# A Conformer and dilated-attention decoder on one core: Silu results moved from PSUM to SBUF, the last feature tile's taps and the weight splits shared out anew

## The chip, the cores and the metric

The kernel runs on one core of a Trainium2 chip. The metric is the time of one execution in microseconds on the device, lower is better. All times below are microseconds (us) unless marked ns. The engines are PE (TensorE; PEld is its weight load), DVE (VectorE), ACT (ScalarE), POOL (GpSimd) and SP, which only issues the DMAs here.

## What is computed

256 tokens of width 2048 go through two layers. Layer 0 is a Conformer convolution layer and a squared-ReLU MLP, layer 1 a dilated attention layer and another MLP; a shared K/V projection stands between them. All in float32. The change touches the convolution layer alone, apart from one scheduling priority that the attention's output product shares:

```python
def conformer_conv(y, w_in, b_in, w_dw, b_dw, ln_g, ln_b, w_out, b_out):
    u = y @ w_in + b_in                      # 2048 -> 4096
    a, gate = jnp.split(u, 2, axis=-1)
    u = a * jax.nn.sigmoid(gate)
    u = depthwise_causal_conv(u, w_dw) + b_dw   # 31 taps per feature
    u = jax.nn.silu(layernorm(u, ln_g, ln_b))
    return u @ w_out + b_out
```

## The kernel before

Everything lies transposed: 128 features on the partitions, the 256 tokens along the free axis, so the width of 2048 is KT = 16 feature tiles. Weights come as 128x2048 tiles of 1 MB, one per output tile. To keep float32 accuracy on the fast float32r path, a weight tile `raw` is split: ACT casts it to `hi` (line 138), DVE or POOL subtracts to get `lo` (line 140). `split_upto(n)` does this for the tiles up to number n of a fixed list `order` (32 tiles of w_in, then 16 of w_out at 32 to 47, then the MLP and so on). The set POOL_LO says whose `lo` POOL makes; the rest is DVE's. The pool `wp` has 11 buffers for raw, hi and lo together, so a new split waits until a product has released an older tile. Activations are split in the same way (`split_into`, lines 219 to 221). A product (`product`, lines 188 to 195) is, per K tile, one 128x512 matmul with `hi` and one 128x256 matmul with `lo`: a pair.

**The convolution stage** (loop over c at line 397). For each feature tile c PE makes two products with w_in, value (`pa`) and gate (`pg`), of 48 matmuls each; ACT makes sigmoid(pg) (line 417), DVE makes u (line 418), and `conv` makes the 31 taps: some products on ACT (line 323) that POOL adds in part (line 332) and DVE sums by TENSOR_REDUCE (line 355), the rest as a chain on DVE (lines 344 to 349). For the last tile, 15, PE takes 18 taps with diagonal matrices (line 311; each matmul is two rows of the trace), ACT 7, DVE 6. `center` subtracts a shift from a finished tile (line 382) and ACT squares it (line 384); `statistics` lets PE sum the columns of tiles and squares (128x1 matmuls, line 236). In iteration c it stands between the value and the gate product. After the last tile come mean, variance and its root, spread over the partitions by four PE transposes (line 247) into `norm`.

**Silu and w_out.** For each c DVE normalizes (lines 477, 478), ACT applies Silu (line 480) into `s`, a tile of the PSUM pool `psp`, which has 8 buffers in all, and `split_into` makes the activation tile. Then `project` multiplies with w_out: the first N0 = 4 output tiles (call them f0 to f3) go together over the first LAST = 13 K tiles, each into its own PSUM tile, so that PE can follow the activations as they come; then each of the four is finished alone over the K tiles left, and its residual add is done on DVE (lines 490, 492), its scaled split on ACT and DVE (lines 226, 227), its sum of squares (lines 258, 262). The other 12 output tiles follow one by one. The attention's w_o goes through the same `project`.

The order on each engine is set by a scheduler at build time, which follows the order of the code and `tc.high_priority`. Each engine then works strictly in that order.

## Time and profile before

| | before |
|---|---|
| median of 3 runs | 2055.55 us (2054.39 to 2055.83) |
| the profiled execution's own time | 2054.33 us |
| its span (first to last instruction) | 2052.1 us |
| busy: PE / PEld / DVE / ACT / POOL | 98% / 87% / 62% / 48% / 11% |
| granted TensorE clock, mean | 0.99 of full |
| DMA, mean over the span | 179 GB/s |

PE is busy for 98% of the span. In the 40 slices of the page only the first, the fifth and the last fall below nine tenths, and the fifth (205 to 257 us) is the lowest, with six: this is where the convolution ends and the product with w_out begins. An idle time in a row stands in square brackets with what ended it. The clock of TensorE has two levels here, 1.00 (2.4 GHz) and 0.50 (1.2 GHz); a value between is a mean over a stretch.

### The profile page before, as it was taken

The page shows a single profiled execution, that of the slowest core. Times are in us where ns is not written, and L with a number is a line of the kernel's source. Part 1 is how long each engine was busy: PE and PEld are TensorE (multiplying, and loading weights), DVE is VectorE, ACT ScalarE, POOL GpSimd, SP SyncE. Part 2 cuts the span into 40 slices and gives each one's busy share as a digit, 9 for nine tenths or more (in the row PEclk, how much of TensorE's full clock was granted, in tenths as well). Part 3 has the DMA queues.
Part 4 walks back from the last instruction along what each step waited for, and adds up shares of the span by engine and source line. Part 5 has one row for each costly group of instructions (what it writes and reads, how often), then busy time and mean ns, then how long its engine had stood idle before and what let it go on. Part 6 is the DMA issues. An engine that isn't in the chain of part 4 may idle for free.

```text
span 2052.1 us, 28638 instructions
## 1 busy us (share of the span) xinstructions
PE 2007.8 (98%) x11958; PEld 1780.7 (87%) x11958; DVE 1281.1 (62%) x1745; ACT 988.3 (48%) x1353; POOL 228.3 (11%) x102
## 2 busy tenths in 40 slices
PE   8999699999999999999999999999999999999997
PEld 7999678888888888888889987888888888888886
DVE  7999666665555555555675565665555555555564
ACT  4888544543453344345454654454344335434452
POOL 2898320000000000000003220000000000000000
PEclk9999799999999999999999999999999999999999
DMA  7454245555555555555555344555555555555551
GB/s 294 146 192 156 68 158 176 201 185 185 188 190 194 187 185 186 188 194 191 185 185 184 145 144 144 185 187 187 195 191 185 185 187 192 191 189 185 187 187 77
DMA packets 51584, 367.42 MB, mean 179 GB/s; under 512 B 5856, under 2 KB 5856, under 8 KB 7552
## 3 DMA queue, kind: packets, MB, share of 16 engines
q1 hardware_dynamic: 51312, 365.60, 51.6%
q8 instruction: 93, 1.52, 0.3%
q14 instruction: 35, 0.29, 0.0%
q10 hardware_dynamic: 144, 0.01, 0.0%
HBM read 363.49 MB, written 2.10 MB: 178 GB/s over the span
## 4 chain that ended last, share of the span: by engine, by line
PE 51%; issue 35%; DVE 2%; ACT 0%; DVEq 0%; POOLq 0%; POOL 0%
PE ps L194 29%; PE ps L195 15%; PE ps L208 1%; PE ps L209 1%; PE ps L210 1%; PE ps L642 0%; DVE lo L140 0%; DVE act L227 0%; PE ps L615 0%; PE ps L614 0%; PE ps L613 0%; PE ps L680 0%; DVE t L262 0%; DVE t L477 0%; DVE t L478 0%
## 5 line engine op out<-in xcount | busy, mean ns | idle before, releaser
L194 PE MATMUL ps<-act,hi 128*128 128x512 f32 x4672 | 1639.1, 395 | 15.4 <-DVE act L221 11.4
L195 PE MATMUL ps<-act,lo 128*128 128x256 f32 x4672 | 1309.7, 281 | 5.3 <-DVE lo L140 3.6
L194 PEld LDWEIGHTS ps<-act,hi 128*128 128x128 f32 x4672 | 876.7, 188 | 219.7 <-DVE act L221 13.1
L138 ACT CAST hi<-raw 128x2048 fp32r<-128x2048 f32 x336 | 640.7, 1909 | 857.1 <-PE ps L194 699.3
L140 DVE TENSOR_TENSOR lo<-raw,hi 128x2048 fp32r<-128x2048 f32 x295 | 678.0, 2298 | 443.0 <-ACT hi L138 441.1
L195 PEld LDWEIGHTS ps<-act,lo 128*128 128x128 f32 x4672 | 884.6, 189 | 7.7 <-DVE lo L140 4.6
L496 DVE TENSOR_TENSOR h<-ps,h 128x256 f32<-128x256 f32 x288 | 119.6, 424 | 195.1 <-PE ps L195 190.9
L140 POOL TENSOR_TENSOR lo<-raw,hi 128x2048 fp32r<-128x2048 f32 x41 | 189.4, 4624 | 142.6 <-ACT hi L138 139.5
L241 POOL TENSOR_TENSOR rc<-ms,neg_half 128x2 f32<-128x2 f32 x5 | 3.6, 728 | 1628.2 <-DVE ms L270 1628.2
L208 PE MATMUL ps<-act,hi 128*128 128x256 f32 x640 | 184.6, 288 | 0.0
L209 PE MATMUL ps<-act,hi 128*128 128x256 f32 x640 | 181.0, 283 | 0.0
L210 PE MATMUL ps<-act,lo 128*128 128x256 f32 x640 | 180.9, 283 | 0.0
L209 PEld LDWEIGHTS ps<-act,hi 128*128 128x128 f32 x640 | 122.5, 191 | 0.5
L208 PEld LDWEIGHTS ps<-act,hi 128*128 128x128 f32 x640 | 122.2, 191 | 0.5
L210 PEld LDWEIGHTS ps<-act,lo 128*128 128x128 f32 x640 | 122.3, 191 | 0.0
L323 ACT ACTIVATE prod<-u,vecs 128x256 f32<-128x256 f32 x217 | 92.4, 517 | 21.3 <-DVE u L418 13.7
L349 DVE SCALAR_TENSOR_TENSOR ps<-u,vecs,ps 128x256 f32<-128x256 f32 x197 | 79.1, 482 | 0.0
L538 ACT ACTIVATE t<-t 128x256 f32<-128x256 f32 x128 | 52.5, 410 | 42.5 <-DVE t L536 42.5
L214 PE MATMUL ps<-act,raw 128*128 128x256 f32 x256 | 57.7, 386 | 6.4 <-DVE act L297 6.4
L214 PEld LDWEIGHTS ps<-act,raw 128*128 128x128 f32 x256 | 49.3, 194 | 13.1 <-DVE act L297 6.4
L221 DVE TENSOR_TENSOR act<-t,act 128x256 fp32r<-128x256 f32 x128 | 53.3, 416 | 7.4 <-ACT act L220 7.4
L200 DVE TENSOR_TENSOR t<-ps,t 128x256 f32<-128x256 f32 x128 | 53.5, 418 | 1.6 <-ACT t L199 1.6
(109 smaller groups left out, 844.4 us busy)
## 6 DMA issues: line engine op xcount, KB each, us to landing
raw<-in_m_in SPq DMA_DIRECT2D x128, 1024.0 KB, 4.8
raw<-in_m_out SPq DMA_DIRECT2D x128, 1024.0 KB, 4.8
raw<-in_w_in SPq DMA_DIRECT2D x31, 1024.0 KB, 4.9
raw<-in_w_out SPq DMA_DIRECT2D x16, 1024.0 KB, 4.8
raw<-in_w_q SPq DMA_DIRECT2D x16, 1024.0 KB, 4.8
raw<-in_w_o SPq DMA_DIRECT2D x16, 1024.0 KB, 4.9
raw<-in_w_k SPq DMA_DIRECT2D x4, 1024.0 KB, 4.9
raw<-in_w_v SPq DMA_DIRECT2D x4, 1024.0 KB, 4.8
```

The costliest lines, as they stand in the source:

```text
L138: nc.scalar.copy(out=hi, in_=raw)
L140: eng.tensor_tensor(out=lo, in0=raw, in1=hi.bitcast(F32), op=ALU.subtract)
L194: nc.tensor.matmul(ps, lhsT=wh, rhs=a.rearrange("p i t -> p (i t)"), start=k == 0, stop=False)
L195: nc.tensor.matmul(ps[:, :T], lhsT=wl, rhs=a[:, 0, :], start=False, stop=k == KT - 1)
L200: nc.vector.tensor_tensor(out=dst, in0=ps[:, :T], in1=dst, op=ALU.add)
L208: nc.tensor.matmul(ps, lhsT=wh, rhs=a[:, 0, :], start=k == 0, stop=False)
L209: nc.tensor.matmul(ps, lhsT=wh, rhs=a[:, 1, :], start=False, stop=False)
L210: nc.tensor.matmul(ps, lhsT=wl, rhs=a[:, 0, :], start=False, stop=k == KT - 1)
L214: nc.tensor.matmul(ps, lhsT=w[:, k * P:(k + 1) * P], rhs=act_of(k), start=k == 0, stop=k == KT - 1)
L323: nc.scalar.activation(out=slot(buf, i), in_=u[:, j:j + T], func=AF.Copy, scale=tap(c, j))
L349: nc.vector.scalar_tensor_tensor(out=a if j < TAPS - 2 else slot(last, i % 2), in0=x, scalar=tap(c, j), in1=a, op0=ALU.mult, op1=ALU.add)
L496: nc.vector.tensor_tensor(out=h[:, f, :], in0=half, in1=h[:, f, :], op=ALU.add)
```

## The change

1. In POOL_LO `range(39)` becomes `range(36)`: the `lo` of tiles 36, 37 and 38 (w_out's f4, f5, f6) goes from POOL to DVE.
2. Tile 15's taps: 16 on PE, 6 on ACT without a POOL add, 9 on DVE (were 18, 7 and 6).
3. From c = 1 on the gate's weight tile is loaded, split and multiplied ahead of the value's, and `statistics` stands behind both products. The set S1_PLAIN (tiles multiplied unsplit) keeps its numbers, so numbers 11 and 28 now name other tiles of the same pairs.
4. `s` comes from the SBUF pool `tp` (7 buffers) and no longer from PSUM.
5. In `project` the splits behind each of the first four tiles get priority 60.
6. For w_out the common K tiles are 11, not 13; for w_o they stay 13.

```diff
@@ constants @@
-POOL_LO = (set(range(39)) - {28}) | set(range(183, 202, 2))
+POOL_LO = (set(range(36)) - {28}) | set(range(183, 202, 2))
-PE_TAPS = {15: (18, [(6, 1)])}
+PE_TAPS = {15: (16, [(6, 0)])}
@@ order of the weights @@
-        order += [(w_in[c], 2 * c not in S1_PLAIN), (w_in[KT + c], 2 * c + 1 not in S1_PLAIN)]
+        pair = [w_in[c], w_in[KT + c]] if c == 0 else [w_in[KT + c], w_in[c]]
+        order += [(w, 2 * c + i not in S1_PLAIN) for i, w in enumerate(pair)]
@@ loop over c @@
+                pg = s1_product(c)
                 pa = s1_product(c)
                 statistics()
-                pg = s1_product(c)
@@ Silu @@
-        s = ps_tile()[:, :T]
+        s = tmp()
         nc.scalar.activation(out=s, in_=z, func=AF.Silu, scale=col("lng", c), bias=col("lnb", c))
@@ project @@
             finish(f, ws[f], pss[f], range(last, KT))
-            split_upto(n_used[0] + LOOK - N0 + f + 1)
+            with tc.high_priority(60):
+                split_upto(n_used[0] + LOOK - N0 + f + 1)
@@ call for w_out @@
-    acts, rms = project(acts, add_bias_residual, "gl0", range(LAST), LAST)
+    acts, rms = project(acts, add_bias_residual, "gl0", range(LAST - 2), LAST - 2)
```

Between lines 87 and 474 the line numbers of the changed kernel are one higher than before.

What the change does to the order, at three places. **PE behind the last product with w_in**, before (line 210 is the product's last matmul, 236 are column sums, of tiles `act` and of squares `t`, 311 the taps of tile 15):

```order
L210 MATMUL ps_2411<-act_475,lo_2287 128x256
L236 MATMUL ps_1888<-ones_d_91,act_2034 128x1 x2
L236 MATMUL ps_1888<-ones_d_91,t_2350 128x1 x2
L236 MATMUL ps_1888<-ones_d_91,t_2501 128x1 x2
L236 MATMUL ps_1888<-ones_d_91,t_2504 128x1 x2
...
L236 MATMUL ps_1888<-ones_d_91,t_2507 128x1 x2
...
L236 MATMUL ps_1888<-ones_d_91,t_2510 128x1 x2
L311 MATMUL ps_2463<-u1_115,act_1864 128x256 x4
```

and in the changed kernel:

```order
L211 MATMUL ps_2398<-act_475,lo_2284 128x256
L237 MATMUL ps_1885<-ones_d_91,t_2341 128x1 x2
L237 MATMUL ps_1885<-ones_d_91,act_2031 128x1 x2
L237 MATMUL ps_1885<-ones_d_91,t_2344 128x1 x2
...
L237 MATMUL ps_1885<-ones_d_91,t_2347 128x1 x2
L237 MATMUL ps_1885<-ones_d_91,t_2497 128x1 x2
L237 MATMUL ps_1885<-ones_d_91,t_2500 128x1 x2
L237 MATMUL ps_1885<-ones_d_91,act_1709 128x1
L312 MATMUL ps_2460<-u1_115,act_1864 128x256 x4
```

Before, the taps stand behind the squares of tiles 8 to 11 (t_2501 to t_2510); now behind those of tiles 8 and 9 only, but also behind sums that stood between the two products of c = 15 before.

**DVE from the u of tile 15 to its finished tile**, before (u0 belongs to tile 14, u1 to tile 15; prod are the ACT products):

```order
L349 SCALAR_TENSOR_TENSOR prod_2304<-u0_114,vecs_73,ps_120 128x256
L355 TENSOR_REDUCE prod_2312<-prod_2304 128x256
L418 SCALAR_TENSOR_TENSOR u1_115<-ps_2352,vecs_73,t_2460 128x256
L355 TENSOR_REDUCE act_2340<-prod_2312 128x256
L344 TENSOR_SCALAR ps_120<-u1_115,vecs_73 128x256
...
L349 SCALAR_TENSOR_TENSOR prod_2482<-u1_115,vecs_73,ps_121 128x256
L355 TENSOR_REDUCE act_2340<-prod_2482 128x256
L358 TENSOR_TENSOR act_2340<-ps_2463,act_2340 128x256
```

and in the changed kernel:

```order
L419 SCALAR_TENSOR_TENSOR u1_115<-ps_2398,vecs_73,t_2457 128x256
L350 SCALAR_TENSOR_TENSOR ps_120<-u0_114,vecs_73,ps_120 128x256
L348 TENSOR_SCALAR ps_121<-u1_115,vecs_73 128x256
...
L350 SCALAR_TENSOR_TENSOR prod_2301<-u0_114,vecs_73,ps_120 128x256
...
L356 TENSOR_REDUCE prod_2309<-prod_2301 128x256
...
L356 TENSOR_REDUCE act_2337<-prod_2309 128x256
...
L356 TENSOR_REDUCE act_2337<-prod_2477 128x256
L359 TENSOR_TENSOR act_2337<-ps_2460,act_2337 128x256
```

The u of tile 15 has moved ahead of three chain steps of tile 14 and of that tile's first TENSOR_REDUCE.

**DVE where f0 to f3 are finished**, before (ps_2704 to ps_2707 are their PSUM tiles):

```order
L490 SCALAR_TENSOR_TENSOR h_75<-ps_2706,vecs_73,h_75 128x256
L227 SCALAR_TENSOR_TENSOR act_2820<-h_75,vecs_73,act_2820 128x256
L492 TENSOR_TENSOR h_75<-ps_2706,h_75 128x256
L490 SCALAR_TENSOR_TENSOR h_75<-ps_2707,vecs_73,h_75 128x256
L492 TENSOR_TENSOR h_75<-ps_2707,h_75 128x256
L227 SCALAR_TENSOR_TENSOR act_2838<-h_75,vecs_73,act_2838 128x256
```

and in the changed kernel (ps_2700 to ps_2703):

```order
L490 SCALAR_TENSOR_TENSOR h_75<-ps_2702,vecs_73,h_75 128x256
L492 TENSOR_TENSOR h_75<-ps_2701,h_75 128x256
L490 SCALAR_TENSOR_TENSOR h_75<-ps_2703,vecs_73,h_75 128x256
L492 TENSOR_TENSOR h_75<-ps_2702,h_75 128x256
L141 TENSOR_TENSOR lo_2809<-raw_2299,hi_2808 128x2048
L228 SCALAR_TENSOR_TENSOR act_2804<-h_75,vecs_73,act_2804 128x256
```

The `lo` of f4 (lo_2809), POOL's before, is now on DVE, behind the line 490 of f3, which reads f3's finished product.

## Rows read from the trace of the kernel before

**Rows 1.** Windows by stage: busy us (count) of PE, PEld, DVE, ACT, POOL; PEclk; DMA.
```profile
50.00:212.50 162.50, 162.50 (x1286) 160.07 (x1285) 156.09 (x293) 137.70 (x259) 143.82 (x67) 1.00 0.46 163
212.50:234.40 21.90, 17.81 (x91) 15.63 (x89) 11.60 (x20) 9.16 (x18) 8.37 (x4) 0.84 0.34 112
234.40:245.70 11.30, 0.00 (x0) 0.00 (x0) 11.23 (x34) 9.84 (x22) 0.00 (x0) 0.51 0.00 0
245.70:271.70 26.00, 25.97 (x129) 21.50 (x129) 8.00 (x21) 8.31 (x15) 1.30 (x1) 0.88 0.05 11
271.70:345.00 73.30, 69.38 (x385) 60.02 (x385) 59.38 (x66) 36.29 (x43) 12.75 (x3) 0.98 0.57 198
```

**Rows 2.** Timeline, 203 to 231 us, all engines: start, us, instruction, [idle before].
```profile
203.88 4.80 DVE L349 SCALAR_TENSOR_TENSOR ps<-u,vecs,ps 128x256 f32<-128x256 f32 x12
...
212.60 0.50 PE L236 MATMUL ps<-ones_d,act 128*128 128x1 f32 x4
...
215.33 0.45 ACT L417 ACTIVATE t<-ps,vecs 128x256 f32<-128x256 f32 x1
...
215.81 0.48 DVE L418 SCALAR_TENSOR_TENSOR u<-ps,vecs,t 128x256 f32<-128x256 f32 x1 [0.26 <-ACT t L417]
216.21 1.74 DVE L355 TENSOR_REDUCE act<-prod 128x256 f32<-128x1536 f32 x1
...
219.96 10.23 PE L311 MATMUL ps<-u,act 128*128 128x256 f32 x36
...
220.84 2.29 DVE L355 TENSOR_REDUCE act<-prod 128x256 f32<-128x2048 f32 x1 [0.15 <-ACT prod L323]
...
230.23 0.42 DVE L358 TENSOR_TENSOR act<-ps,act 128x256 f32<-128x256 f32 x1 [7.11 <-PE ps L311]
```

**Rows 3.** Timeline, 234 to 247 us, start of the product with w_out.
```profile
234.39 0.42 DVE L477 TENSOR_TENSOR t<-act,ps 128x256 f32<-128x256 f32 x1 [0.55 <-PE ps L247]
...
235.90 0.37 ACT L220 CAST act<-ps 128x256 fp32r<-128x256 f32 x1
...
236.31 0.42 DVE L221 TENSOR_TENSOR act<-ps,act 128x256 fp32r<-128x256 f32 x1
...
245.73 0.79 PE L194 MATMUL ps<-act,hi 128*128 128x512 f32 x1 [11.37 <-DVE act L221]
...
246.72 0.79 PE L194 MATMUL ps<-act,hi 128*128 128x512 f32 x1
```

**Rows 4.** Groups of instructions, 0 to 330 us: the same cast read from SBUF.
```profile
L220 ACT CAST act<-act 128x256 fp32r<-128x256 f32 x16 | 5.1, 400 | 0.5 <-DVE act L405 0.5
```

**Rows 5.** Windows of 2 us: TensorE while tile 15's taps run.
```profile
222.00:224.00 2.00, 2.00 (x7) 1.55 (x6) 1.12 (x1) 0.10 (x1) 0.00 (x0) 0.50 0.84 356
```

**Rows 6.** Timeline of DVE, 262 to 345 us.
```profile
271.04 4.19 DVE L227 SCALAR_TENSOR_TENSOR act<-h,vecs,act 128x256 fp32r<-128x256 f32 x1
...
279.89 4.85 DVE L262 TENSOR_TENSOR t<-t 128x256 f32<-128x256 f32 x1
...
286.97 2.28 DVE L140 TENSOR_TENSOR lo<-raw,hi 128x2048 fp32r<-128x2048 f32 x1
...
311.53 0.48 DVE L490 SCALAR_TENSOR_TENSOR h<-ps,vecs,h 128x256 f32<-128x256 f32 x1 [0.69 <-PE ps L195]
...
339.46 0.48 DVE L490 SCALAR_TENSOR_TENSOR h<-ps,vecs,h 128x256 f32<-128x256 f32 x1 [0.69 <-PE ps L195]
```

**Rows 7.** Timeline of POOL, 262 to 345 us.
```profile
270.40 14.05 POOL L140 TENSOR_TENSOR lo<-raw,hi 128x2048 fp32r<-128x2048 f32 x3 [36.75 <-ACT hi L138]
```

**Rows 8.** Timeline of PE, 262 to 300 us: its three waits.
```profile
272.88 0.50 PE L194 MATMUL ps<-act,hi 128*128 128x512 f32 x1 [1.00 <-ACT hi L138]
275.00 0.39 PE L195 MATMUL ps<-act,lo 128*128 128x256 f32 x1 [1.62 <-POOL lo L140]
...
289.31 0.38 PE L195 MATMUL ps<-act,lo 128*128 128x256 f32 x1 [1.30 <-DVE lo L140]
```

**Rows 9.** Timeline of PE, 1250 to 1260 us: product with w_o.
```profile
1254.34 0.39 PE L195 MATMUL ps<-act,lo 128*128 128x256 f32 x1 [2.35 <-DVE lo L140]
```

## The prediction, made before the changed kernel was run

> **What bounds the kernel now.** I read the busy shares by stage first. From 50 to 212.5 us PE is busy all the time at full clock, and so is nearly DVE (156.1 of 162.5 us) [rows 1]; there nothing can be won but by less work. The next two stages, the end of the convolution and the start of the product with w_out, are different: PE is busy 17.8 of 21.9 us and then 0 of 11.3 us, and in that second stretch its clock is the lower level, 0.51 [rows 1]. In the two after them, the product with w_out, PE is busy but for 3.9 us of waits, at clocks of 0.88 and 0.98 [rows 1]. After 345 us PE is the bound again, save one short stretch at w_o. So a gain must come from 212.5 to 345 us, and what matters there is which wait ends last.
>
> I then read the timeline of that stretch, step by step.
>
> *The tail of the convolution.* The sigmoid of tile 15 starts on ACT at 215.33, u on DVE at 215.81, and PE's taps run from 219.96 for 10.23 us, partly at the lower clock (0.50 from 222 to 224 us) [rows 2, 5]. DVE has done its part before and waits 7.11 us for those taps, until 230.23 [rows 2]. PE's taps set the end here.
>
> *The start of w_out.* The first normalizing step runs at 234.39, and the first activation tile is ready when line 221 ends, at 236.31 + 0.42 = 236.73 [rows 3]. Yet PE starts only at 245.73, after 11.37 us of idling that a line 221 on DVE ended [rows 3]. That is not the first line 221 but the tenth: one activation takes 0.99 us, the distance of PE's first two starts (245.73 and 246.72) [rows 3], and 236.73 + 9 x 0.99 = 245.64. The cause is in the code. `psp` has 8 buffers; `norm` holds one, the 16 tiles `s` go around in the other 7, and f0's PSUM tile, which comes after them, takes the buffer of s number 9 (counted from 0), f1's that of number 10, and so on. So PE waits for a buffer, not for data.
>
> *The product with w_out.* Three waits stand here, 1.00, 1.62 and 1.30 us, for `hi`, for POOL's `lo` and for DVE's `lo` [rows 8]. While POOL makes its three `lo` in 14.05 us [rows 7], two DVE steps last 4.19 and 4.85 us [rows 6] that otherwise take about 0.45.
>
> **The change, part by part.**
>
> *Gate first, sums behind both, taps shared anew (edits 2 and 3).* The sigmoid no longer waits for the last product. DVE now reaches u with three chain steps and one TENSOR_REDUCE fewer ahead of it, as the order shows. A chain step costs 4.80 / 12 = 0.40, the long TENSOR_REDUCE 2.29 [rows 2], and 0.26 us of waiting for the sigmoid goes: 215.81 - 0.26 - 3 x 0.40 - 2.29 = 212.1. PE must have finished too: its last product ended by 212.60, and the six column sums (12 matmuls, 0.50 / 4 = 0.125 each [rows 2]) that stood between the two products now stand behind: 212.6 - 1.5 = 211.1. So u starts at 212.1. Behind it DVE has 12 small steps (three of tile 14, nine of tile 15, since its chain grows from 6 taps to 9), 4.8 us, TENSOR_REDUCEs of 2.29, 1.74 and 2.29, and one centering of 0.42: 11.5 us [rows 2]. With 0.4 for u itself, the last TENSOR_REDUCE ends at 224.0. PE's part: 15 column-sum matmuls from 211.1, 1.9 us, and then 16 taps, at worst at the old mean of 10.23 x 16 / 18 = 9.1 us: 222.1. So DVE, not PE, is late next, and the tail is 230.23 - 224.0 = 6.2 us shorter. PE will then have idled some microseconds and may do the last sums and transposes at half clock; I take off 0.5 (12 matmuls at 0.125 more would be 1.5, but most of them wait for data anyway). **Gain 5.7.** Bounds: if u comes as late as now, only the two taps go, 10.23 x 2 / 18 = 1.1; if DVE, which waited for sigmoids before, reaches u as early as PE allows, 7.2. I take the middle way, nearest to the rows of DVE. The ACT products and POOL's adds of tile 15 shrink too; they are hidden, since the last TENSOR_REDUCE needs them some 9 us after u.
>
> *Silu in SBUF (edit 4).* f0's PSUM tile no longer has to wait for an `s`, so PE starts when the first activation is ready: 245.73 - 236.73 = **9.0 gained**. What cover is needed: PE must not run into the activations. PE's four pairs per K tile take 4 x 0.349 = 1.40 us (0.349 from the five output tiles between 311.53 and 339.46, 27.93 / 5 = 5.59 each, 16 pairs [rows 6]), the activations come every 0.99, so PE stays behind. And f1 to f3 no longer start 0.99 apart but one pair apart, about 0.70 at half clock: 3 x 0.29 = **0.9 gained**. The lower clock at the start stays, since PE idles ahead of it in both kernels. `z` and `s` now share 7 buffers, 3.5 tiles deep at 0.99 each, 3.5 us, against 2.34 us from the first step to line 221 [rows 3]: no wait.
>
> What speaks against edit 4: the cast of an activation takes 0.37 us when it reads PSUM [rows 3] and 0.40 when it reads SBUF [rows 4], 0.03 more per tile, for the first tile alone on PE's path. By the Trainium skill, "ScalarE: Activation LUTs", section "Step-by-step: what each stage is for", ScalarE writes faster to PSUM than to SBUF, so that this edit would move Silu to the slower side; it gives no figure, no row here shows a Silu into SBUF, and the sum by it would be the same but for the first tile's Silu.
>
> *Splits of f4 to f6 on DVE, priority, 11 common K tiles (edits 1, 5, 6).* From 271.7 to 345 us PE needs 12 x 5.59 = 67.0 and takes 73.3 [rows 1, 6]: 3.9 of waits and 2.4 that are mostly half clock after the longest of them. With 11 common tiles f0's weights come free 6 pairs (2.1 us) earlier against f3's end, so `hi` of f4 is ready in time. But the order puts f4's `lo` behind f3's line 490 on DVE: f3's end, then 0.48 + 0.42 + 2.28 = 3.2 us [rows 6], of which two hi matmuls cover about 0.4. A wait of 2.8 takes the place of 1.00 + 1.62, so it is 0.2 worse, and the half clock behind it stays. The third wait, 1.30, should go, since POOL no longer holds DVE up (three `lo` cost DVE 3 x 2.28 = 6.8, the two held steps alone gave 8.1 away). **Gain 1.1.** Bounds: all 6.3 if the scheduler's order hurts less than I read it; 2 lost if f5 or f6 waits as well.
>
> *w_o.* Edit 5 acts there too; a wait of 2.35 for DVE's `lo` stands there [rows 9], and the order of `lo` moves by one short step. I take 0, between 1 gained and 1 lost.
>
> **Sum:** 5.7 + 9.0 + 0.9 + 1.1 = 16.7 us. The profiled execution's own time of 2054.33 (span 2052.1) becomes 2037.6; it lies 1.2 under the median of the three runs, 2055.55, which becomes **2038.9 us**.
>
> **The rivals.**
>
> *u stays late.* ACT's queue could still hold the sigmoid behind a cast that waits for a weight buffer, as it does now. Then the tail gains 1.1 only: 1.1 + 9.0 + 0.9 + 1.1 = 12.1, 2043.5 us. Against it: the gate's product now ends a whole product earlier.
>
> *PE's wait is not for the buffer.* If something else releases it, the 9.9 of edit 4 fail and 6.8 remain: 2048.8. Against it: the 0.99 steps of PE's first starts [rows 3].
>
> *POOL holds DVE in the Silu loop.* Line 222 now has both inputs in SBUF, like the two steps that stretched to 4.19 and 4.85 beside POOL [rows 6, 7]. If POOL's last `lo` of the stage slides into the loop, one line 222 waits up to 14.05 / 3 = 4.7: gain 12.0, 2043.6. Against it: the last activation's weights were split long before 234 us, POOL being busy 8.4 us in that stage [rows 1], and f4's split is no longer POOL's. By the Trainium skill, "SBUF — State Buffer", section "Who interferes with whom", a DVE instruction with two SBUF inputs and a GpSimd instruction that reads SBUF shut each other out; the two stretched rows agree.
>
> *Slower.* With the gate first, ACT's queue may stop at every sigmoid until the gate's product is done, and the casts behind it come late. POOL, which splits most of those weights, has 162.5 - 143.8 = 18.7 us of slack over 14 tiles, 1.3 each [rows 1]. If ACT stops for half a product (162.5 / 28 = 5.8, half 2.9) per tile, PE loses 14 x 1.6 = 22.4: 2061.3, slower than before. It decides from 1.3 + 16.7 / 14 = 2.5 us per tile. Against it: splits run two tiles ahead of PE, and ACT is idle 24.8 us in that stretch [rows 1].
>
> **How the numbers follow.** My forecast has 0.70, u late 0.15, POOL in the loop 0.05, the other release 0.04, slower 0.04, something outside 0.02. A measurement of this kernel can tell about 0.2%, 4.1 us, from no change. All cases but the slower one and mishaps together gain more: faster 0.92, same 0.04, slower 0.04. The range runs from the upper bounds nearly summed (7.2 + 9.0 + 0.9 + 6.3 + 1 = 24.4, 2031.2) to just beyond u late and POOL in the loop: 2031.5 to 2045.
>
> **What would show it.** u of tile 15 near 212, taps done before DVE's last TENSOR_REDUCE, that ending near 224; the first pair of w_out about 2.4 us behind the first normalizing step, near 231; one wait of some 2.8 us for f4's `lo`, and no second. Wrong would be a PE that waits between 50 and 212 us, or a first pair later than 3 us behind the first normalizing step.

## The result, and the profile after

The changed kernel takes **2043.08 us** (median of 4 runs, 2040.53 to 2045.01); the kernel before took 2055.01 in the runs beside it (2054.39 to 2055.83). The ratio is 0.9942, 95% interval 0.9930 to 0.9953: 11.9 us are gone. In the two profiled executions 2054.33 became 2042.95 and the span 2052.1 became 2041.1, 11.0 us less; those 11.0 are followed through the trace here. The runs of the changed kernel also lie further apart than those of before, 4.5 us against 1.4.

Windows by stage, the changed kernel: busy us (count) of PE, PEld, DVE, ACT, POOL, then PEclk, DMA share, GB/s. They answer to [rows 1].

```profile
50.00:212.50 162.50, 160.59 (x1266) 157.94 (x1266) 155.25 (x291) 139.25 (x263) 143.64 (x67) 1.00 0.46 163
212.50:220.00 7.50, 7.50 (x46) 7.05 (x46) 6.51 (x12) 5.94 (x9) 6.92 (x2) 0.73 0.42 142
220.00:235.00 15.00, 12.31 (x61) 10.65 (x60) 8.34 (x16) 1.06 (x3) 1.00 (x2) 0.73 0.29 93
235.00:261.00 26.00, 24.54 (x129) 21.09 (x129) 19.24 (x51) 18.09 (x35) 0.00 (x0) 0.91 0.03 7
261.00:334.00 73.00, 70.94 (x396) 61.69 (x396) 56.05 (x71) 38.58 (x45) 0.00 (x0) 0.98 0.60 210
```

Of the 11.37 us in which PE did nothing ahead of w_out, 2.58 are left. Two things are new: PE is busy 160.59 of 162.50 us from 50 to 212.5, where it never waited before, and the clock is 0.73 in both stretches from 212.5 to 235, where it was 0.84 until the first normalizing step.

The tail of the convolution on DVE (timeline: start, us, instruction, idle before with what ended it), to be read against [rows 2, 3]. From line 88 on to line 474 the changed kernel's numbers are one higher.

```profile
213.78 0.48 DVE L419 SCALAR_TENSOR_TENSOR u<-ps,vecs,t 128x256 f32<-128x256 f32 x1 [0.99 <-PE ps L211]
...
223.57 2.29 DVE L356 TENSOR_REDUCE act<-prod 128x256 f32<-128x2048 f32 x1
227.32 0.42 DVE L359 TENSOR_TENSOR act<-ps,act 128x256 f32<-128x256 f32 x1 [1.46 <-PE ps L312]
...
231.23 0.16 DVE L451 COPY mu<-ps 128x2 f32<-128x2 f32 x1 [3.03 <-PE ps L237]
...
233.77 0.42 DVE L477 TENSOR_TENSOR t<-act,ps 128x256 f32<-128x256 f32 x1 [1.01 <-PE ps L248]
```

The same stretch on PE:

```profile
213.51 0.50 PE L237 MATMUL ps<-ones_d,t 128*128 128x1 f32 x4
...
217.49 9.79 PE L312 MATMUL ps<-u,act 128*128 128x256 f32 x32
...
236.31 0.80 PE L195 MATMUL ps<-act,hi 128*128 128x512 f32 x1 [2.58 <-DVE act L222]
```

u starts at 213.78 (before 215.81), the last add of the convolution at 227.32 (before 230.23), the first normalizing step at 233.77 (before 234.39). Of 2.9 us that the taps' end gained, 0.6 are left at the end of the stage. But PE's first pair of w_out now stands 2.54 us behind that step, where it stood 11.34 behind [rows 3].

The new wait in the convolution stage, on PE, and what DVE does ahead of it:

```profile
77.92 0.70 PE L440 MATMUL ps<-act,ones_s 128*128 128x256 f32 x2 [1.91 <-DVE act L356]
```

```profile
72.99 3.22 DVE L350 SCALAR_TENSOR_TENSOR ps<-u,vecs,ps 128x256 f32<-128x256 f32 x8
76.12 1.75 DVE L356 TENSOR_REDUCE act<-prod 128x256 f32<-128x1536 f32 x1
```

In the trace of before the same TENSOR_REDUCE runs ahead of those eight steps:

```profile
72.94 1.74 DVE L355 TENSOR_REDUCE act<-prod 128x256 f32<-128x1536 f32 x1
```

In w_out PE and DVE, and DVE's last add of that stage; they answer to [rows 6, 8]:

```profile
263.12 0.50 PE L195 MATMUL ps<-act,hi 128*128 128x512 f32 x1 [2.00 <-ACT hi L139]
```

```profile
261.35 2.28 DVE L141 TENSOR_TENSOR lo<-raw,hi 128x2048 fp32r<-128x2048 f32 x1
```

```profile
332.69 0.42 DVE L492 TENSOR_TENSOR h<-ps,h 128x256 f32<-128x256 f32 x1
```

The last add in the trace of before:

```profile
345.57 0.42 DVE L492 TENSOR_TENSOR h<-ps,h 128x256 f32<-128x256 f32 x1
```

PE waits 2.00 us for a `hi`. Counted in PE's order it is f5's: behind the 128 matmuls of f0 to f3 come f4's first with `hi` (at 260.63, nearly without a wait), then f5's first with `hi` (at 263.12) and only then f4's first with `lo`. The 1.00 of [rows 8] is f5's `hi` as well. f4's `lo`, made on DVE from 261.35 to 263.63, comes just in time for its matmul at 263.69. The two other waits of [rows 8] are gone. The last add of w_out stands at 332.69; in the trace of before it stands at 345.57. So the account of the two executions is:

| stretch | before | after | gain | predicted |
|---|---|---|---|---|
| to the first normalizing step | 234.39 | 233.77 | 0.62 | 5.7 |
| from there to the first pair of w_out | 11.34 | 2.54 | 8.80 | 9.0 |
| from there to the last add of w_out | 99.84 | 96.38 | 3.46 | 0.9 + 1.1 |
| from there to the end of the span | 1706.5 | 1708.4 | -1.9 | 0 |
| sum | | | 11.0 | 16.7 |

The first line has starts, the others differences of the starts named; for the changed kernel 233.77, 236.31 - 233.77, 332.69 - 236.31 and 2041.1 - 332.69.

In w_o the wait for a `hi` part is longer, 3.71 us where the trace of before has 2.25, and the granted clock is down to 0.89 in the 16 us around it. It is 0.89 in a second stretch too, but there it falls in the trace of before as well (0.66 from 1254 to 1258 us):

```profile
1211.75 0.50 PE L195 MATMUL ps<-act,hi 128*128 128x512 f32 x1 [3.71 <-ACT hi L139]
```

The same wait in the trace of before:

```profile
1222.52 0.50 PE L194 MATMUL ps<-act,hi 128*128 128x512 f32 x1 [2.25 <-ACT hi L138]
```

The clock of the changed kernel in both stretches:

```profile
1206.00:1222.00 16.00, 12.29 (x62) 10.36 (x61) 7.88 (x18) 8.36 (x25) 0.00 (x0) 0.89 0.31 116
1238.00:1254.00 16.00, 12.83 (x64) 10.70 (x64) 14.84 (x22) 12.05 (x13) 0.00 (x0) 0.89 0.66 244
```

### The profile page after: what moved, and what is told of

Same layout as the page of the kernel before. It is cut to its first block, busy times and chain, and to the rows that moved or that the text cites. A ratio compares the mean times of both kernels' runs of the same rounds, so it can differ in the third digit from the quotient of the medians.

```text
span 2041.1 us, 28646 instructions
## 1 busy us (share of the span) xinstructions
PE 2008.0 (98%) x11954; PEld 1781.6 (87%) x11954; DVE 1279.8 (63%) x1751; ACT 987.9 (48%) x1350; POOL 213.8 (10%) x98
## 4 chain that ended last, share of the span: by engine, by line
PE 56%; issue 35%; DVE 5%; ACT 2%; POOL 0%; DVEq 0%; POOLq 0%; ACTq 0%
PE ps L195 30%; PE ps L196 15%; PE ps L209 2%; PE ps L210 2%; PE ps L211 2%; ACT hi L139 1%; DVE lo L141 1%; DVE ps L350 1%; PE ps L215 1%; PE ps L237 1%; DVE act L222 1%; ACT act L652 1%; PE ps L312 0%; ACT act L657 0%; PE ps L616 0%
## 5 line engine op out<-in xcount | busy, mean ns | idle before, releaser
L141 DVE TENSOR_TENSOR lo<-raw,hi 128x2048 fp32r<-128x2048 f32 x298 | 685.3, 2300 | 444.3 <-ACT hi L139 443.4
L141 POOL TENSOR_TENSOR lo<-raw,hi 128x2048 fp32r<-128x2048 f32 x38 | 175.7, 4626 | 108.1 <-ACT hi L139 106.0
L222 DVE TENSOR_TENSOR act<-t,act 128x256 fp32r<-128x256 f32 x144 | 60.1, 417 | 8.3 <-ACT act L221 8.3
L221 ACT CAST act<-t 128x256 fp32r<-128x256 f32 x144 | 58.6, 407 | 0.8
```

The lines of the kernel that those rows point to most:

```text
L141: eng.tensor_tensor(out=lo, in0=raw, in1=hi.bitcast(F32), op=ALU.subtract)
L222: nc.vector.tensor_tensor(out=a[:, 1, :], in0=src, in1=a[:, 0, :].bitcast(F32), op=ALU.subtract)
```

## The experiments

Three questions were open: is the buffer really what PE waited for; where the tail's 5 us went; and which edit made w_out shorter. Each kernel has four timed runs or more beside the kernel before; the ratio to it, with its 95% interval, is given each time. An interval is about 2.4 us wide to either side, so single edits are told apart by the stage in the trace first, and by medians only where they differ by more. A trace shows one execution, not always the median one. The line numbers of these kernels differ by up to four.

**1. The Silu results alone** (kernel before, one line):

```diff
-        s = ps_tile()[:, :T]
+        s = tmp()
```

> The kernel before with the Silu results in SBUF and nothing else changed. Theory B (PE's first w_out pair waited for a PSUM buffer that an s held): the first pair comes 2.4 to 2.6 us behind the first normalizing step, near 237.0 instead of 245.73, f1 to f3 start back to back, and the time falls by about 9.5 us to 2045.5 (2044.5 to 2047). Rival T (the first pair came early because the convolution's tail and the splits around it were shortened): the pair stays near 245 and the time within 1.5 us of 2055.

Measured: 2045.40 us, 0.9954 (0.9941 to 0.9966). The first pair on PE, and the first normalizing step on DVE:

```profile
238.70 0.80 PE L194 MATMUL ps<-act,hi 128*128 128x512 f32 x1 [2.56 <-DVE act L221]
```

```profile
236.18 0.42 DVE L477 TENSOR_TENSOR t<-act,ps 128x256 f32<-128x256 f32 x1 [0.55 <-PE ps L247]
```

2.52 us lie between them instead of 11.34: 8.8 gained, as in the changed kernel. Theory B holds. (The convolution's end was 1.8 us later here than in the trace of before, with the same order on every engine until then: the 18 taps took 10.65 us, not 10.23.) But from the first pair to the last add of w_out it takes 99.82 us, as before: f1 to f3 start closer together and the third wait of [rows 8] is gone, but the wait for f5's `hi` grows from 1.00 to 2.00 and the granted clock behind it is lower (0.95 from 261 to 334).

**2. The changed kernel with the Silu results back in PSUM** (the same line the other way).

> The changed kernel with the Silu results back in PSUM. Theory B: the first w_out pair is late again by about 9 us (near 245 instead of 236.31) and the time is 2052.5 (2051 to 2054). Rival T: the pair stays within 1 us of 236.3 and the time between 2043 and 2045.

Measured: 2047.30 us, 0.9962 (0.9950 to 0.9975). The wait is back in full, 11.35 us behind the first normalizing step at 233.56:

```profile
244.91 0.80 PE L195 MATMUL ps<-act,hi 128*128 128x512 f32 x1 [11.38 <-DVE act L222]
```

Yet the time rises by 4.2 us only, not by 9, and the expectation was missed by 5. The stage tells why: from the first pair to the last add 93.34 us pass here, against 96.38 in the changed kernel, and PE does not wait once in between. The scheduler's order on PE differs behind the common K tiles. Here each of f0 to f3 has its last five pairs in one piece, so f0's weights come free 15 pairs ahead of f3's end, and the casts of f4's and f5's `hi` (from 265.31, until 269.74) are done before PE asks for them. In the changed kernel the last pairs of the four are dealt out in turn, f0's own last one stands 5 pairs ahead of f3's end, and the first cast starts at 258.66, 1.8 us before PE is done with f3; f4's `hi` is just ready, f5's, the next on ACT, is 2 us late. So the earlier start gives some 3 us back at the next wait. Another 1.9 us lie behind w_out: from its last add to the end 1706.5 us pass here, 1708.4 in the changed kernel. Gains of this kind don't add.

**3. The tail's edits alone** (kernel before with edits 2 and 3).

```diff
-PE_TAPS = {15: (18, [(6, 1)])}
+PE_TAPS = {15: (16, [(6, 0)])}
-                pa = s1_product(c)
-                statistics()
-                pg = s1_product(c)
+                pg = s1_product(c)
+                pa = s1_product(c)
+                statistics()
```

(and the weights' order of edit 3)

> The kernel before with the tail edits alone: 16 taps on TensorE and 6 products on ScalarE, gate product first, column sums behind both products. Prediction's account (DVE sets the end of the convolution's tail): the first normalizing step comes at about 228.7 instead of 234.39 and the time falls by 5.7 us to 2049.3. Theory S (column sums ahead of the taps take 4 us and leave the taps at half clock; a wait of 1.9 us near 78 appears): the first normalizing step within 1 us of 234 and a time of 2054.4 (2053.5 to 2056).

Measured: 2052.97 us, 0.9986 (0.9977 to 0.9994; runs from 2050.50 to 2055.48). DVE:

```profile
232.81 0.42 DVE L478 TENSOR_TENSOR t<-act,ps 128x256 f32<-128x256 f32 x1 [0.73 <-PE ps L248]
```

2.9 us by the ratio: neither 5.7 nor 0.6, with the first normalizing step at 232.81; both sides missed. The wait of 1.9 us near 78 is there, and in this execution the clock fell to 0.50 behind it, so that u comes at 215.43. Nearer to theory S, but it needed experiment 4 to be understood.

**4. The taps alone** (kernel before with edit 2 and nothing else).

> The kernel before with the taps of the last tile alone shared out anew (16 on TensorE, 6 products on ScalarE). Theory Q (with fewer products, the sigmoid no longer stands behind a cast on ScalarE, so u comes early without the gate going first): sigmoid near 213.2 instead of 215.33, u near 213.7 instead of 215.81, taps at full clock in about 7.1 us, the first normalizing step near 231.3 instead of 234.39, and 2052 (2051 to 2053.2). Rival: u stays near 215.8 and only the two taps' 1.1 us go: 2054 (2053.3 to 2055).

Measured: 2048.76 us, 0.9966 (0.9954 to 0.9979), more than either side expected. The sigmoid on ACT, then DVE:

```profile
213.15 0.48 ACT L417 ACTIVATE t<-ps,vecs 128x256 f32<-128x256 f32 x1 [1.36 <-PE ps L210]
```

```profile
213.66 0.48 DVE L418 SCALAR_TENSOR_TENSOR u<-ps,vecs,t 128x256 f32<-128x256 f32 x1 [1.32 <-ACT t L417]
...
226.22 0.43 DVE L358 TENSOR_TENSOR act<-ps,act 128x256 f32<-128x256 f32 x1
...
230.87 0.42 DVE L477 TENSOR_TENSOR t<-act,ps 128x256 f32<-128x256 f32 x1 [1.01 <-PE ps L247]
```

and PE's taps:

```profile
215.34 8.84 PE L311 MATMUL ps<-u,act 128*128 128x256 f32 x32
```

u starts at 213.66 **without** the gate going first. With the POOL add and one product gone from tile 15, the scheduler put the sigmoid ahead of the cast that stood before it (215.33 in [rows 2]). The first normalizing step comes 3.5 us earlier, and w_out is 2.6 shorter as well (97.21 us from the first pair; its third wait is gone). The taps did not run at full clock, as theory Q had it: they took 8.84 us, not 7.1. That cost nothing here, as DVE's last TENSOR_REDUCE ends later still and the last add (226.22) waits for no one else. Theory Q holds for the sigmoid and u, not for the taps; its sum missed the part in w_out.

**5. The changed kernel with the old order of products** (edit 3 undone).

> The changed kernel with the old order of the products in the convolution stage (value, column sums, gate). Prediction's account (gate first brings u and with it the taps forward): u near 215.8, the first normalizing step some 3 us later than in the changed kernel (near 236.5) and a time of 2046 (2045 to 2047.5). Theory S (what u gains, the column sums and the wait of 1.9 us near 78 take away): no wait of PE between 50 and 212, the first normalizing step within 1 us of 233.8, and a time of 2043 (2041.5 to 2044.5).

Measured: 2039.63 us, 0.9923 (0.9911 to 0.9936): **faster than the changed kernel**, by 3.9 us going by the two ratios, and below the range that theory S gave. PE:

```profile
212.98 0.50 PE L236 MATMUL ps<-ones_d,act 128*128 128x1 f32 x4
...
215.38 7.16 PE L311 MATMUL ps<-u,act 128*128 128x256 f32 x32
...
233.86 0.79 PE L194 MATMUL ps<-act,hi 128*128 128x512 f32 x1 [2.58 <-DVE act L221]
```

Only 10 column-sum matmuls (20 records) stand ahead of the taps here, not 15; the taps begin at 215.38 and run at full clock (7.16 us, where the changed kernel's took 9.79), and the first normalizing step comes at 231.32. No wait stands between 50 and 212. The full clock is the luck of this execution: experiment 4's kernel has the same order on PE, DVE and ACT up to the Silu loop, and its taps took 8.84. It did not set the end either, as in both DVE's last TENSOR_REDUCE does (adds at 226.26 and 226.22). Experiments 3 and 4 say the same of edit 3 from the other side: edits 2 and 3 together are 4.1 us slower, by the ratios, than edit 2 alone. The two intervals overlap slightly in either pair; both pairs agree, and in the traces 1.9 to 2.5 us of it stand at the first normalizing step. **Edit 3 costs time, with the other edits and without them: some 2 us in the traces of the tail, about 4 by the ratios.** Where the rest lies is not assigned.

**6. The column sums behind the taps** (changed kernel, the sums of the last tile held in program order).

```diff
-                statistics()
+                if c < KT - 1:
+                    statistics()
...
+            if keep:
+                tc.keep_in_program_order(m)
```

(`m` is each column-sum matmul of the last call of `statistics`)

> The changed kernel with TensorE's 16 taps of the last tile put ahead of the waiting column sums, by holding those sums in program order behind the taps. Theory S (it is the column sums ahead of them that lower the clock): the taps begin at about 214.3 at a granted clock of 1.00, take 4.9 to 5.5 us and are done before 220; DVE's last reduce (225.9) then sets the last add of the convolution (226 instead of 227.32), the first normalizing step comes near 232.0 and the time is about 2041.4 (2040.5 to 2042.5). Rival C (the clock falls whatever stands there, as the product's end and the wait for u leave PE idle): the taps take 9.8 us at half clock until 224.1, all column sums come behind them, the first normalizing step near 235 and a time of 2044.5 (2043.5 to 2046).

Measured: 2042.44 us, 0.9935 (0.9922 to 0.9949). PE:

```profile
214.61 7.18 PE L314 MATMUL ps<-u,act 128*128 128x256 f32 x32 [0.65 <-DVE u L422]
...
234.81 0.79 PE L195 MATMUL ps<-act,hi 128*128 128x512 f32 x1 [2.58 <-DVE act L222]
```

The clock stays at 1.00 through the taps, 7.18 us where the changed kernel needed 9.79; all the sums then follow without a gap until 229.7, the clock falling in their last part, and the first normalizing step stands at 232.27 (expected 232.0). Theory S holds against C in this trace, though 7.18 is more than the 4.9 to 5.5 I expected at full clock. All traces taken together bear it out: in 11 of the 12 with sums ahead of the taps the taps took longer than at full clock (8.55 to 10.14 us for 16, 10.23 and 10.65 for 18), experiment 5's being the twelfth, and in neither of the two with the taps first (this one and experiment 12). The tail gained what was expected (1.5 us). But the profiled execution, 2038.83 us, is the fastest of the five, 3.6 below their median; the medians, 0.6 apart, don't separate.

**7. The mean's matmul one tile later** (changed kernel; the wait near 78 alone).

```diff
-nc.tensor.matmul(pmean[:, :T], lhsT=ones_s, rhs=v_of(c - 2), start=c == 2, stop=c == SHIFT + 1)
+for i in [k for k in (c - 3, c - 2) if k >= 0 and (k == c - 3 or c == SHIFT + 1)]:
+    nc.tensor.matmul(pmean[:, :T], lhsT=ones_s, rhs=v_of(i), start=i == 0, stop=i == SHIFT - 1)
```

> The changed kernel with the mean's matmul issued one tile later and nothing else. Theory W (the wait of 1.9 us near 78 is lost time): no wait of PE between 50 and 212, last w_in product at about 211.6, u near 211.9, and 2041.2 (2040 to 2042.3). Rival K (time won ahead of the column sums is lost there again, as taps and sums run at a lower clock for longer): the first normalizing step within 0.5 us of 233.8 and 2042.5 to 2044.

Measured: 2041.31 us, 0.9926 (0.9914 to 0.9938). DVE:

```profile
212.00 0.48 DVE L419 SCALAR_TENSOR_TENSOR u<-ps,vecs,t 128x256 f32<-128x256 f32 x1 [0.59 <-PE ps L211]
...
221.40 2.29 DVE L356 TENSOR_REDUCE act<-prod 128x256 f32<-128x2048 f32 x1
225.53 0.42 DVE L359 TENSOR_TENSOR act<-ps,act 128x256 f32<-128x256 f32 x1 [1.84 <-PE ps L312]
...
232.30 0.42 DVE L478 TENSOR_TENSOR t<-act,ps 128x256 f32<-128x256 f32 x1 [1.01 <-PE ps L248]
```

PE waits nowhere between 50 and 212, its last w_in product ends at 211.74, u starts at 212.00 and DVE's last TENSOR_REDUCE ends at 223.69. These are nearly the prediction's own numbers, 211.1, 212.1 and 224.0. Even so DVE then waits 1.84 us for PE's taps, and column sums fill the time to 229.76. 1.5 of the 1.9 us reach the first normalizing step. W holds in the trace; the medians (1.8 us apart) lean its way but lie within their uncertainty.

**8. to 11. The three edits of w_out.** Undone in the changed kernel: (8) all three, (9) the 11 common K tiles alone, (10) the `lo` taken from POOL alone, (11) the priority alone.

```diff
-POOL_LO = (set(range(36)) - {28}) | set(range(183, 202, 2))
+POOL_LO = (set(range(39)) - {28}) | set(range(183, 202, 2))
-            with tc.high_priority(60):
-                split_upto(n_used[0] + LOOK - N0 + f + 1)
+            split_upto(n_used[0] + LOOK - N0 + f + 1)
-    acts, rms = project(acts, add_bias_residual, "gl0", range(LAST - 2), LAST - 2)
+    acts, rms = project(acts, add_bias_residual, "gl0", range(LAST), LAST)
```

> The changed kernel with the three edits of w_out's first tiles undone (POOL's share of the lo parts, the priority of the splits, 13 common K tiles). From the first w_out pair to the last of w_out's adds the changed kernel takes 96.4 us, and the kernel with only the Silu results moved took 99.8: theory B gives 99.8 here too. Whether w_o's new wait of 3.7 us for a hi part comes from these edits is open: if so, 1.9 us come back there and the time is 2044.7 (2043.5 to 2046); if not, 2046.6 (2045.5 to 2048).

> The changed kernel with 13 common K tiles again in w_out's first four output tiles, the other edits kept. Theory L (the fourth tile's hi and lo parts need the buffers of the first tile's, which come free 6 pairs of matmuls, about 3.9 us, earlier with 11 common tiles): PE's waits for f4's hi and lo grow from 4.3 us by 3 to 4 us, w_out takes 99.5 to 100 us from the first pair, and the time is 2046.5 (2045 to 2048). Rival P (it is the lo parts taken from POOL that shorten this stretch): the waits stay within 1 us and the time is 2043 to 2044.2.

> The changed kernel with the lo parts 36 to 38 on POOL again, priority and 11 common tiles kept. Theory P (these three on DVE are what shortens the stretch between the first pair and w_out's last add, 96.4 us in the changed kernel, 98.7 with the three edits undone): POOL's lo ends f4's wait again, 98.3 to 99 us, and 2045 (2044 to 2046.5). Rival R (the priority of the splits does it): 96 to 97 us and 2042 to 2044.

> The changed kernel without the priority of the splits in the first four tiles. Theory P: 96 to 97 us from the first pair to w_out's last add, and 2041.5 to 2044. Rival R: 98 to 99 us and 2044.5 to 2046.5. In w_o the other order of splits may shorten or lengthen the wait of 3.7 us for a hi part: open, within 2 us.

| undone in the changed kernel | time, us | ratio (95%) | first pair to last add of w_out |
|---|---|---|---|
| nothing | 2043.08 | 0.9942 (0.9930 to 0.9953) | 96.38 |
| all three | 2043.36 | 0.9943 (0.9931 to 0.9956) | 98.66 |
| 13 common K tiles | 2041.15 | 0.9933 (0.9920 to 0.9947) | 96.02 |
| POOL's `lo` | 2041.51 | 0.9933 (0.9921 to 0.9945) | 98.49 |
| priority | 2042.20 | 0.9935 (0.9922 to 0.9947) | 96.02 |

In the stage the answer is plain: the 2.1 to 2.5 us hang on POOL's `lo` alone (P against R and L); the kernel without priority, with the changed kernel's order there, differs by 0.36. With it PE waits for POOL again, for f4's `lo`:

```profile
261.04 0.54 PE L195 MATMUL ps<-act,hi 128*128 128x512 f32 x1 [2.00 <-ACT hi L139]
263.15 0.58 PE L196 MATMUL ps<-act,lo 128*128 128x256 f32 x1 [1.57 <-POOL lo L141]
```

and DVE, beside POOL's three `lo` (258.57 to 272.57), has three short steps with both big inputs in SBUF stretched to over 4 us each:

```profile
259.26 4.12 DVE L228 SCALAR_TENSOR_TENSOR act<-h,vecs,act 128x256 fp32r<-128x256 f32 x1
...
263.63 4.46 DVE L228 SCALAR_TENSOR_TENSOR act<-h,vecs,act 128x256 fp32r<-128x256 f32 x1
268.01 4.84 DVE L263 TENSOR_TENSOR t<-t 128x256 f32<-128x256 f32 x1
```

In the changed kernel no step of DVE in w_out but the `lo` themselves is longer than 0.6 us. The Trainium skill, "SBUF — State Buffer", section "Who interferes with whom", says that such a DVE instruction and a GpSimd instruction that reads SBUF shut each other out; these rows agree on DVE's side, where steps of 0.42 to 0.48 us are held for over 4.

Theory L fell: with 13 common tiles f4's `hi` is cast at the same distance from the first pair (22.15 us, 22.35 with 11), and the wait of 2.00 us for f5's stays. (The 4.3 us in its expectation were a misreading: 2.3 of them are the `lo` wait of w_o.) With the Silu results in SBUF the scheduler deals the last pairs of f0 to f3 out in turn whatever the number of common tiles, and f0's last pair stands 5 pairs ahead of f3's end in both orders; with `s` in PSUM it stands 9 pairs ahead with 13 common tiles (the kernel before) and 15 with 11 (experiment 2). In the total none of the three edits can be seen: all five medians lie within 2.2 us, (8) and (9) below both of their ranges and (10) below the 2044 to 2046.5 that P gave; (11) lies in P's range.

Why not, the run without priority shows. Its order is the changed kernel's up to the end of w_out, on PE, ACT and DVE, and still its first normalizing step comes 2.3 us earlier. Windows of 2 us (PEclk stands ahead of the last two columns), first of the changed kernel, then of the one without priority, and PE's taps and first pair in the latter:

```profile
216.00:218.00 2.00, 2.00 (x10) 1.97 (x10) 2.00 (x3) 2.00 (x6) 2.00 (x1) 0.50 0.86 360
218.00:220.00 2.00, 2.00 (x6) 1.58 (x5) 2.00 (x4) 1.65 (x2) 2.00 (x1) 0.50 0.03 8
220.00:222.00 2.00, 2.00 (x6) 1.55 (x6) 2.00 (x4) 0.00 (x0) 0.29 (x1) 0.50 0.54 86
222.00:224.00 2.00, 2.00 (x9) 1.69 (x8) 1.83 (x5) 0.42 (x1) 0.00 (x0) 0.79 0.88 369
```

```profile
216.00:218.00 2.00, 2.00 (x11) 1.91 (x11) 2.00 (x3) 2.00 (x6) 2.00 (x1) 0.63 0.87 369
218.00:220.00 2.00, 2.00 (x6) 1.55 (x6) 2.00 (x4) 1.69 (x3) 2.00 (x1) 0.52 0.04 12
220.00:222.00 2.00, 2.00 (x11) 1.75 (x10) 2.00 (x4) 0.00 (x0) 0.33 (x1) 1.00 0.49 70
```

```profile
217.11 8.55 PE L312 MATMUL ps<-u,act 128*128 128x256 f32 x32
...
234.01 0.79 PE L195 MATMUL ps<-act,hi 128*128 128x512 f32 x1 [2.58 <-DVE act L222]
```

The clock falls in both within the column sums, but by these rows it stays down for about 6.8 us in the changed kernel's execution and for 3.4 in the other, so the same 16 taps take 9.79 us in the first and 8.55 in the other. Two executions of one order differ by 2.3 us at the first normalizing step, and in these rows by nothing but the clock. It may be a good part of the spread of 4.5 us between the changed kernel's runs; only one of them was traced, so that is not shown. The kernel before, with its runs 1.4 apart here, differs in the same way by 1.8 us (experiment 1).

**12. A version from these findings.** The changed kernel with experiments 6 and 7 in it, and 14 taps on PE instead of 16.

> The changed kernel with the column sums of the last tile behind the taps, 14 taps on TensorE instead of 16, and the mean's matmul issued one tile later. Theory: no wait near 78 (1.9 us), taps about 6.1 us, column sums until 228.6 less 1.9, the first normalizing step near 229.5, and a time of 2036 (2034 to 2038.5). Rival: DVE, with two taps more, sets the end and nothing is won at the taps: first normalizing step near 230.4 to 231 and 2038.5 to 2040.5.

Measured: **2035.45 us**, 0.9902 (0.9888 to 0.9915), 19.8 us below the kernel before and about 8 below the changed one going by the ratios; its interval and the changed kernel's don't overlap. PE:

```profile
212.38 6.31 PE L314 MATMUL ps<-u,act 128*128 128x256 f32 x28 [0.65 <-DVE u L422]
...
232.31 0.79 PE L195 MATMUL ps<-act,hi 128*128 128x512 f32 x1 [2.58 <-DVE act L222]
```

The taps run from 212.38 at full clock, the sums follow, and the first normalizing step stands at 229.77 (expected 229.5), 4.0 us ahead of the changed kernel's. The rival was half right: the last four sums wait 0.74 us for DVE, whose last TENSOR_REDUCE ends at 224.30, so DVE does set the end, but earlier than the rival had it. The span of the profiled execution is 9.3 us below the changed kernel's. Of the other 5.3 us 1.5 lie in w_out (94.85 us from the first pair, against 96.38) and 3.8 behind it: from its last add (327.16) to the end of the span 1704.6 us pass, against 1708.4. The expectation had no price for either, so that its total was met is partly luck. The order in w_o is another, with a `hi` wait of 2.22 us (at 1204.08), and the clock does not fall there at all:

```profile
1200.00:1262.00 62.00, 56.20 (x310) 46.99 (x309) 36.77 (x57) 32.47 (x57) 0.00 (x0) 1.00 0.39 141
```

## Why the prediction was right and wrong

The time lies in the range, but not because the sum held. Of the 16.7 us 11.0 came in the profiled executions: 0.2 less at the buffer, 5.1 less in the tail, 1.9 lost in w_o, and 1.5 more in w_out, partly for another reason than the one given. That 2043.1 stands next to the 2043.5 of the rival "u stays late" is chance, as u came 2.0 us earlier. And the sign that I named for being wrong, "a PE that waits between 50 and 212 us", came.

**Right: PE's wait was for the buffer.** The step "245.73 - 236.73 = 9.0 gained" measured 8.80, in the changed kernel and alone (experiments 1 and 2). The condition that PE stays behind the activations held, though an activation now comes every 1.14 us (16 Silus from 234.77 to 251.94) and not every 0.99. Silu and cast cost 67 ns of that on ACT (Silu 602 ns into SBUF, 569 into PSUM; cast 406 and 372 ns), and in DVE's new order line 478 stands directly behind the line 477 that it reads, 0.45 us after it, where steps stood 0.33 apart before. The step "3 x 0.29 = 0.9 gained" measured 0.89: f0 to f3 start within 2.09 us (236.31 to 238.40), before within 2.98 (245.73 to 248.71). The Trainium skill, "ScalarE: Activation LUTs", section "Step-by-step: what each stage is for", says that ScalarE writes faster to PSUM than to SBUF; the trace agrees, with 33 ns of a Silu of 128x256.

**Wrong in size: the tail, 0.62 instead of 5.7.** Four steps of it failed:
- *"PE must have finished too ... 211.1."* PE's wait of 1.91 us that ended at 77.92 was for a TENSOR_REDUCE. Edit 3 moved that instruction behind eight more chain steps in DVE's order, and the mean's matmul stands in PE's queue ahead of the next product. I looked for the order only around tile 15. Without that wait (experiment 7) 211.7, 212.0 and 223.7 were measured for the 211.1, 212.1 and 224.0 of the sum.
- *"15 column-sum matmuls from 211.1, 1.9 us."* They took 4.0 us (213.51 to 217.49). An x4 in the timeline is two matmuls with two records each, as the 32 records of the 16 taps show; I priced a matmul with the time of one record. (The sums that moved away from between the products were taken as 12 matmuls; they are 12 records, six matmuls, and took 1.26 us in the trace of before, so that the 1.5 there came out near.)
- *"So DVE, not PE, is late next."* DVE's last TENSOR_REDUCE ended at 225.86, PE's taps after 227.2; the clock had fallen within the column sums, and "at worst at the old mean ... 9.1" was 9.79. In the same order with a shorter fall (experiment 11) DVE was late, as I said: its TENSOR_REDUCE ended at 225.90 and the add came at 226.00.
- *"I take off 0.5 (... most of them wait for data anyway)."* The column sums moved behind both products stand partly behind the taps too: from the last add to `mu` it takes 3.91 us, before 2.08, and 0.46 more goes to the half clock of what follows. That is 2.3, not 0.5. With the last add 2.9 us earlier instead of 6.2, this makes the 5.1 us that the tail is short.

The rival "u stays late" did not come true, nor did ACT's queue stall at the gate. The fear behind the slower rival was right in one way, at the wrong place: going gate first does cost PE time, not 22 us by ACT but 2 to 4, by DVE's order, the sums and the clock. And the credit I gave to the gate going first for an early sigmoid belongs to edit 2 (experiment 4).

**Too small: w_out, 3.46 instead of 0.9 + 1.1.** "A wait of 2.8 takes the place of 1.00 + 1.62" was a wait of 2.00, and the trace puts it down to `hi`, not to `lo`. Both ended together: f4's `lo` was done 3.15 us behind f3's end (260.48 to 263.63), as priced (3.2), and f5's `hi` 0.56 us before it. Only the cover was too small: the two `hi` matmuls ahead of f4's `lo` took 0.50 us each, not 0.4 in all. f4's `hi` was ready in time, but not by "f0's weights come free 6 pairs earlier": that held only for `s` in PSUM (15 pairs ahead in experiment 2, 9 in the order of before, 5 here) and was undone by edit 4 in the same change. "The third wait, 1.30, should go" held. Taking `lo` off POOL is worth 2.1 to 2.5 us where 1.1 was said; the rest, about 1, is of the size of the 0.89 at the start of f0 to f3.

**w_o, -1.9 instead of 0 (within 1).** The wait for `hi` grew by 1.5 us and the clock is lower behind it, where it stayed at 1.00 before. In the kernel with Silu in PSUM that wait is 3.53 us and the clock falls behind it too, but it stays at 1.00 in the second stretch and nothing is lost (1706.5 us from w_out's last add to the end); in experiment 12 the wait is 2.22, the clock falls in neither stretch and 1.9 are gained. So both count. The long wait takes edits 1 and 3 together: it is 2.24 and 2.25 without edit 1 (experiments 10 and 8) and 2.25 without edit 3 (experiment 5). In the first stretch the clock goes with the order: in the five traces (before, experiments 3, 4, 5 and 12) whose PE has a further wait of 0.3 to 0.4 us behind that for `hi`, it stays at 1.00, in the other nine it falls. In the second it differs without such a sign; why stays open in both.

**POOL beside DVE in the Silu loop.** POOL was idle there and no step on line 222 was held up, as forecast; the stretched steps of experiment 10 show what edit 1 took away.

## What to carry to other kernels

An edit that reorders work for one tile reorders a list-scheduled program everywhere: read the order over the whole stage and count what then stands ahead of each engine's next long job, before costing the place that you meant to change. Gains on either side of one buffer chain don't add: freeing PE 9 us earlier was worth 9 with the old splits and 4 with the new, as it reordered PE and brought back a wait that the new splits alone did not have (f5's weights, 3 us with the clock behind it), and 1.9 us at w_o. A trace is one execution: look how far two traces of one order lie apart before you explain a difference of 2 us. And keep long runs of 128x1 matmuls behind the work that needs the clock, not ahead of it, where that work sets the end.

## What the runs showed of the hardware

- A column sum, an fp32 matmul with one moving column, takes 0.22 us of PE at full clock (22 of them from 221.63 to 226.46 in experiment 6), half as much as a tap of 256 columns (7.18 / 16 = 0.45).
- TensorE's granted clock fell from 1.00 to 0.50 within such a run of sums although PE was busy all the time (2.00 of 2.00 us in each window above); ahead of the fall PE had multiplied 256 columns at a time, and then one. When it fell and rose again differed between executions of the same order: it was down for 6.8 and 3.4 us in the changed kernel's, and in experiment 5's it did not fall until the taps were done, where with the same order in experiment 4's it was down as they began (taps of 7.16 and 8.84 us).
- A Silu of 128x256 takes 33 ns more into SBUF than into PSUM (602 and 569 ns), and the cast that reads it 34 ns more from SBUF (406 and 372).
- A DVE step of 128x256 with both big inputs in SBUF, 0.42 to 0.48 us otherwise, took 4.12 to 4.84 us beside POOL's three `lo` of 128x2048, 14.00 us together (experiment 10).
